# One token tile first through four weight pieces, at two hand-overs of a two-block transformer kernel

## The chip, the cores and the metric

The kernel runs on one core of a Trainium2 chip. The metric is the device time of one execution in microseconds (us). Times of one profiled execution come from the hardware profiler; its engines are PE (TensorE, matrix products and transposes), PEld (its weight loads), DVE (VectorE), ACT (ScalarE), POOL (GpSimd) and SP (SyncE, which issues the transfers).

## The reference

256 tokens of width 1024 go through two blocks. All of it is float32; the kernel splits each operand into a high and a low part and forms three products, so that the result keeps float32 accuracy.

```python
def first_block(...):                        # two layers
    for l in range(DEPTH):
        xn = rms_norm(h, norm_g[l])
        ... = jnp.split(xn @ w_in[l], offsets, axis=-1)
        branches = (dsa_branch(...), mla_branch(...), diff_branch(...), sgu_branch(...), memory_branch(...))
        mixed = sum(sigmoid(merge[:, :, n]) * ((o * silu(gates[:, :, n])) @ w_branch[l, n]) ...)
        h = h + mixed @ w_out[l]
    return rms_norm(h, final_norm_g)

def second_block(x, c, ...):
        ada = c_act @ w_ada[l] + b_ada[l]
        shift_a, scale_a, gate_a, shift_m, scale_m, gate_m = jnp.split(ada, N_ADA, axis=-1)
        h = modulate(rmsnorm(x, g_mix[l]), shift_a, scale_a)
        gq, gk, gv, gr, gg, mq, mk, mv = jnp.split(h @ w_in[l], IN_SPLITS, axis=-1)
        o_gla = ...   # gated linear attention from gq, gk, gv, gr, gg
        o_moba = ...  # block-sparse attention from mq, mk, mv
        x = x + gate_a * (concatenate([o_gla, o_moba], axis=-1) @ w_out[l])
        h = modulate(rmsnorm(x, g_mlp[l]), shift_m, scale_m)
        x = x + gate_m * (square(relu(h @ w_ff1[l])) @ w_ff2[l])
    return rmsnorm(x, g_final)
```

The two places where a new operand needs whole rows of a sum (a norm over 1024 columns) between two weight products are called hand-overs here. Hand-over 1: the product with `w_out` of layer 2, the residual, two norms in a row, and the first product of block 2. Hand-over 2: the product with `w_out_2`, the gated residual, a norm, and the first product with `w_ff1_2`.

## The kernel before

**Pieces.** All weights stream as pieces of 512 rows (4 slices of 128 along K) by up to 512 columns, 1 MB each. SP loads a piece into one of three raw buffers (`load`, L357). `split` (L369 to L389) makes a high part on ACT (L381) and a low part on DVE (L382), each as two half-splits of 128 x 1024; there are four buffers of each kind. `run_stream` splits a piece three pieces ahead of its use and loads it six ahead. With `late` it splits after the piece's matmuls instead of before.

**Units.** The 256 tokens are two token tiles: tile 0 (tokens 0 to 127) and tile 1. `mm_tok` (L427) multiplies one tile with one piece: four products hi x hi (L431) and four with the low part of the weights (L432) in turn, then four with the low part of the tokens (L434), 12 matmuls of 512 columns into one PSUM bank. This is called a unit. A chunk of 512 output columns needs two pieces (K halves) for each of the two tiles, four units.

**The order of units.** An ordinary `chunk` or `chunk_pair` runs both tiles of a piece before the next piece. At the hand-overs the kernel before has two other orders. `chunk_pair(..., by_tile=True)`, for `w_out` of layer 2 (L1224) and `w_out_2` (L1626), runs the first two pieces (first K half, both chunks) in the ordinary order and then the second K half as: chunk 0 tile 0, chunk 1 tile 0, chunk 0 tile 1, chunk 1 tile 1. `chunk_by_tile`, for the first chunk behind each hand-over (gq and gk at L1596, the first 512 columns of `w_ff1_2` at L1708), runs K half 0 tile 0, K half 1 tile 0, then both halves of tile 1. The second 512 columns of `w_ff1_2` are made transposed (`chunk_tr`, L444 to L447, matmuls of 256 columns) and need no transposes; the first are transposed by PE afterwards (L552).

**From rows to operand.** At hand-over 1 a unit's residual is L1183, at hand-over 2 L1608 and L1609; ACT takes the square sum of each half row (`sumsq`, L629); DVE makes the reciprocal root in small steps (L225 to L233) and scales the rows (L1282). `to_operand_mod` (L585) then transposes 8 squares (L552), scales and shifts two of four on ACT (L597) and two on DVE (L595), and splits into high (L598, ACT) and low part (L599, DVE). The gated operand inside `w_out_2` goes through `to_operand` (L566 ACT, L567 DVE).

**What sets the order.** PE, ACT and DVE each run their instructions in the order that the program fixes. That order comes from a scheduler that sees the code's order and priorities (`urgent`, L1287's `SOONER`); `defer(fn, n)` (L311) places work after n more units, and `half` (L315) counts them.

Of the kernel before, what the change touches and what calls it, by code (L numbers as in the profile page):

```python
# [57 lines left out]
def block_kernel(ctx: ExitStack, tc: tile.TileContext, a, out):  # L58
# [414 lines left out]
    def chunk_by_tile(ap, ops, c0, n, evac, pre=None, post=None, mid=None):  # L473

        st = {}

        def f0(hi, lo):
            st["w"] = hi, lo
            st["ps"] = [mbank(), mbank()]
            assert 0 in ops[0]().filled  # L480
            mm_tok(st["ps"][0], ops[0](), 0, hi, lo, 4, n, True, False, 0)
            half(0)

        def f1(hi, lo):
            w = [st["w"], (hi, lo)]
            mm_tok(st["ps"][0], ops[1](), 0, hi, lo, 4, n, False, True, 0)
            evac(0, st["ps"][0][:, :n])
            half(1)
            if mid:
                mid()  # L490
            for j in range(2):
                assert 1 in ops[j]().filled
                mm_tok(st["ps"][1], ops[j](), 0, *w[j], 4, n, j == 0, j == 1, 1)
                if j == 1:
                    evac(1, st["ps"][1][:, :n])
                    if post:
                        post()
                half(j)
# [1276 lines left out]
```

## Time and profile before

| | |
|---|---|
| median of three runs | 1231.11 us (1230.07 to 1232.33) |
| profiled execution | 1232.42 us |
| its span | 1230.5 us |
| PE busy | 1211.6 us, 98% of the span |
| DVE busy | 903.7 us, 73% |
| ACT busy | 664.5 us, 54% |
| mean granted PE clock | 0.99 |
| transfers | 231.30 MB, 188 GB/s on average |

A row of the timeline has a start in us from the start of the span, a duration, the engine, the line, the operation and the names of its output and inputs, and in brackets how long the engine stood idle before and what ended that. Successive matmuls overlap in these rows: the distance between starts, not the duration, is what one costs. "x4" is a run of four. Hand-over 1 lies at about 887 to 917 us, hand-over 2 at about 1020 to 1052 us.

### The profile page before, as it was taken

Reading aid. Unit: us, or ns where it says so; the run is one execution under the profiler, and the core shown is the slowest. Engines: PE = TensorE matmul, PEld = TensorE weight load, DVE = VectorE, ACT = ScalarE, POOL = GpSimd, SP = SyncE. Lnnn points to the kernel's source line nnn. Section 1 sums busy time; section 2 is a strip of 40 time slices with the busy share of each in tenths; the row PEclk is TensorE's granted clock in tenths of the full one; section 3 lists DMA queues with packets and bytes.
Section 4 is the critical chain, followed back from the end, with each engine's and each line's share of the span. In section 5 each row is a group of like instructions: output and inputs, shape, how many; then the busy total and the mean of one; then the engine's idle time right before and its main releaser. Section 6 shows DMA issues by size and latency. Waiting matters only on the chain.

```text
span 1230.5 us, 17201 instructions
## 1 busy us (share of the span) xinstructions
PE 1211.6 (98%) x6497; PEld 1044.2 (85%) x6497; DVE 903.7 (73%) x1887; ACT 664.5 (54%) x1161; POOL 14.8 (1%) x35
## 2 busy tenths in 40 slices
PE   9999999999999999999999999999999999999997
PEld 7799888898888888898888988888878877899995
DVE  6866778768896777776887788876685877757665
ACT  6744645567465455546444756555455655545442
POOL 3000000000000000000000000000000000000000
PEclk9999999999999999999999999999988999999999
DMA  8855465544566465755565535656357724757650
GB/s 303 306 181 199 137 206 189 178 153 156 163 220 205 138 206 186 250 172 171 171 211 192 172 124 189 206 172 218 109 171 265 255 85 163 223 188 243 233 174 35
DMA packets 121284, 231.30 MB, mean 188 GB/s; under 512 B 5421, under 2 KB 17009, under 8 KB 121073
## 3 DMA queue, kind: packets, MB, share of 16 engines
q1 hardware_dynamic: 120880, 230.12, 56.8%
q8 instruction: 51, 0.84, 0.3%
q14 instruction: 33, 0.26, 0.1%
q0 software_dynamic: 320, 0.08, 0.1%
HBM read 229.10 MB, written 2.63 MB: 188 GB/s over the span
## 4 chain that ended last, share of the span: by engine, by line
PE 91%; DVE 4%; ACT 1%; DMA 1%; issue 1%; SPq 0%; ACTq 0%
PE pm L431 22%; PE pm L432 22%; PE pm L434 22%; PE pm L446 3%; PE pm L444 3%; PE pm L447 3%; PE po L703 3%; PE pm L552 3%; DVE wl L382 2%; PE pm L683 2%; DMA wt<-in_w_in_dram 1%; PE pm L1100 1%; PE pm L988 1%; PE pm L851 1%; PE po L434 1%
## 5 line engine op out<-in xcount | busy, mean ns | idle before, releaser
L382 DVE TENSOR_TENSOR wl<-wt,wh 128x1024 fp32r<-128x1024 f32 (+3 forms) x386 | 443.3, 1175 | 174.2 <-ACT wh L381 173.6
L381 ACT ACTIVATE wh<-wt 128x1024 fp32r<-128x1024 f32 (+3 forms) x386 | 379.5, 1019 | 272.1 <-PE pm L434 168.0
L431 PE MATMUL pm<-wh,hi 128*128 128x512 f32 (+4 forms) x1320 | 521.0, 396 | 4.0 <-ACT hi L598 2.6
L432 PE MATMUL pm<-wl,hi 128*128 128x512 f32 (+4 forms) x1320 | 509.5, 387 | 0.0
L434 PE MATMUL pm<-wh,lo 128*128 128x512 f32 (+4 forms) x1320 | 348.0, 384 | 0.0
L431 PEld LDWEIGHTS pm<-wh,hi 128*128 128x128 f32 x1320 | 251.3, 190 | 52.6 <-ACT hi L598 4.7
L432 PEld LDWEIGHTS pm<-wl,hi 128*128 128x128 f32 x1320 | 251.3, 190 | 45.6 <-DVE wl L382 0.6
L434 PEld LDWEIGHTS pm<-wh,lo 128*128 128x128 f32 x1320 | 246.5, 189 | 47.5
L446 PE MATMUL pm<-lo,wh 128*128 128x256 f32 x352 | 99.8, 284 | 2.9 <-DVE lo L580 2.9
L444 PE MATMUL pm<-hi,wh 128*128 128x256 f32 x352 | 100.6, 286 | 0.0
L447 PE MATMUL pm<-hi,wl 128*128 128x256 f32 x352 | 99.6, 284 | 0.0
L656 ACT ACTIVATE w<-w,s 128x256 f32<-128x256 f32 (+1 forms) x112 | 49.9, 446 | 39.0 <-DVE s L653 39.0
L446 PEld LDWEIGHTS pm<-lo,wh 128*128 128x128 f32 x352 | 67.8, 193 | 3.6 <-DVE lo L580 3.1
L444 PEld LDWEIGHTS pm<-hi,wh 128*128 128x128 f32 x352 | 67.9, 193 | 0.3
L447 PEld LDWEIGHTS pm<-hi,wl 128*128 128x128 f32 x352 | 67.7, 192 | 0.1
L1332 DVE SCALAR_TENSOR_TENSOR w<-wt,cact,w 128x512 f32<-128x512 f32 x84 | 62.7, 747 | 1.7 <-DMA wt<-in_w_ada_dram 0.6
L1146 ACT ACTIVATE t<-pm,s 128x512 f32<-128x512 f32 x40 | 27.5, 688 | 43.6 <-PE pm L434 43.6
L703 PEld LDWEIGHTS po<-t,w 128*128 128x128 f32 x352 | 46.0, 191 | 2.9
L552 PE MATMUL pm<-ident,t 128*128 128x128 f32 (+1 forms) x332 | 43.8, 273 | 1.6 <-DVE t L1282 1.6
L703 PE MATMUL po<-t,w 128*128 128x64 f32 (+1 forms) x352 | 44.8, 270 | 0.0
L552 PEld LDWEIGHTS pm<-ident,t 128*128 128x128 f32 (+1 forms) x332 | 38.4, 137 | 7.4 <-issue 2.4
L629 ACT ACTIVATE j<-t 128x512 f32<-128x512 f32 (+3 forms) x60 | 28.8, 479 | 28.1 <-DVE t L1682 14.1
(282 smaller groups left out, 1005.1 us busy)
## 6 DMA issues: line engine op xcount, KB each, us to landing
wt<-in_w_in_dram SPq DMA_DIRECT2D x99, 1024.0 KB, 5.0
wt<-in_w_ff_dram SPq DMA_DIRECT2D x32, 1024.0 KB, 5.4
wt<-in_w_ada_dram SPq DMA_DIRECT2D x24, 1024.0 KB, 5.2
wt<-in_w_branch_dram SPq DMA_DIRECT2D x20, 1024.0 KB, 5.1
wt<-in_w_out_dram SPq DMA_DIRECT2D x12, 1024.0 KB, 5.1
wt<-in_mem_w_kv_dram SPq DMA_DIRECT2D x8, 1024.0 KB, 7.3
wt<-in_w_in_dram SPq DMA_DIRECT2D x4, 904.0 KB, 5.5
wt<-in_w_in_dram SPq DMA_DIRECT2D x4, 768.0 KB, 4.4
```

Source lines behind the costliest of these rows:

```text
L381: pin(A.activation(hv[:, ks], wv[:, ks], AF.Copy), on)
L382: pin(V.tensor_tensor(lv[:, ks], wv[:, ks], hv[:, ks].bitcast(F32), OP.subtract), on)
L431: T.matmul(ps[:, :n], xh, hi[:, i, :n], start=first and i == 0, stop=False)
L432: T.matmul(ps[:, :n], xh, lo[:, i, :n], start=False, stop=False)
L434: T.matmul(ps[:, :n], xo.lo[:, k0 + i, tsl(t)], hi[:, i, :n], start=False, stop=last and i == nk - 1)
L444: T.matmul(ps, wh, xh, start=first and i == 0 and c % 2 == 0, stop=False, skip_group_check=True)
L446: T.matmul(ps, wh, xl, start=False, stop=False, skip_group_check=True)
L447: T.matmul(ps, wl, xh, start=False, stop=last and i == nk - 1, skip_group_check=True)
L552: T.transpose(ps[:, i, :], src[:, i * w:(i + 1) * w], ident)
L656: A.activation(p[:, k, :], p[:, k, :], AF.Exp, bias=mx[:, k:k + 1], scale=-1.0, accum_out=sm[:, k:k + 1])
L703: T.matmul(opsum[t][:, h, :], pt[:, k * nb + b, :], u["v"](h, b), start=b == 0, stop=b == nb - 1)
L1332: V.scalar_tensor_tensor(acc, w[:, i, :], B["c"][:, k:k + 1], acc, op0=OP.mult, op1=OP.add)
```

## The change

Both special orders go. `chunk_pair` gets an `order` of its four pieces; with it, tile 0 goes through all four (both K halves and both chunks), with four units, and the pieces stay in their four split buffers (`keeps`). Then tile 1 goes through the four in the order chunk 0 (both K halves), chunk 1 (both). After each of tile 1's first three units `freed` lets the stream split the next piece. This order is used for `w_out` of layer 2, for gq/gk together with mq in block 2 (so mq moves ahead of the narrow gg), for `w_out_2`, and for the first 1024 columns of `w_ff1_2`; the second 512 of these are now made by tiles and transposed like the first. `modulated` is deferred by five units (it was 3 for tile 0 and 2 for tile 1 at hand-over 1, and 2 at hand-over 2).

```diff
+        at = dict(split=1, load=AHEAD, live=1)
+        def more(i):
+            while at["split"] < min(i + LOOK + 1, N):
+                raw = pieces[at["split"]][5]
+                if not raw and at["live"] > LOOK:
+                    break
+                at["live"] += not raw
+                split(at["split"])
+                at["split"] += 1
+            while at["load"] < min(at["split"] + AHEAD - LOOK, N):
+                load(at["load"])
+                at["load"] += 1
+        def freed():
+            at["live"] -= 1
+            more(at["i"])
+        stream["freed"] = freed
...
-            if i + LOOK < N and not late:
-                split(i + LOOK)
-            if i + AHEAD < N:
-                load(i + AHEAD)
+            _, nk, n, fn, pre, raw, keeps = pieces[i]
+            more(i)
...
-            if i + LOOK < N and late:
-                split(i + LOOK)
+                if not keeps:
+                    at["live"] -= 1
...
+        todo = order or [(j, q) for j in range(2) for q in range(2)]
+        for k, (j, q) in enumerate(todo):
+            def fn(hi, lo, j=j, q=q, k=k):
+                mm(j, q, 0, hi, lo)
+                if not order:
...
+                st["w", j, q] = hi, lo
+                half(k % 2)
+                if k < 3:
+                    return
+                for m, jq in enumerate([(0, 0), (1, 0), (0, 1), (1, 1)]):
+                    mm(*jq, 1, *st["w", *jq])
+                    if m < 3:
+                        stream["freed"]()
+                    elif post:
+                        post()
+                    half(m % 2)
...
-                   pres={(0, 0): lambda: defer(lambda: mixT(1), 1)}, by_tile=l == DEPTH - 1)
+        def second_half():
+            for t in range(2):
+                defer(lambda t=t: mixT(1, (t,)), 1 + t)
+        chunk_pair(a["w_out"][l], mt, [(0, 512), (512, 512)], [eo(0), eo(1)], pres={(0, 0): second_half},
+                   order=[(0, 0), (0, 1), (1, 0), (1, 1)] if l == DEPTH - 1 else None)
...
-            x[t], x[t], rsqrt(m, 1), None, op0=OP.mult)), 3 - t)
+            x[t], x[t], rsqrt(m, 1), None, op0=OP.mult)), 5)
...
-        chunk_by_tile(w2, ops, 0, 512, tok("gqk", 512), pre=block2_begins)
+        chunk_pair(w2, ops, [(0, 512), (1552, 512)], [tok("gqk", 512), tok("mq", 512)], pres={(0, 0): block2_begins},
+                   order=[(0, 0), (0, 1), (1, 0), (1, 1)])
         chunk(w2, ops, 1536, 16, tok("gg", 16), post=lambda: lanes[1].add(gla()))
-        chunk(w2, ops, 1552, 512, tok("mq", 512))
...
-                    defer(modulated(t, r, B["x2"], B["am"], B["bm"]), 2)
+                    defer(modulated(t, r, B["x2"], B["am"], B["bm"]), 5)
...
-                   by_tile=True)
+                   order=[(0, 0), (0, 1), (1, 0), (1, 1)])
...
-        chunk_by_tile(w1, fo, 0, 512, ff1_0)
+        chunk_pair(w1, fo, [(0, 512), (512, 512)], [ff1_by_tile(0), ff1_by_tile(1)],
+                   order=[(0, 0), (0, 1), (1, 0), (1, 1)])
         for f in range(8):
-            if f + 1 < 8:
+            if 0 < f < 7:
                 ff1(f + 1)
             ff2(f)
-            if f == 0:
-                after_norm.update(id(p) for p in pieces[first + 2:first + 4])
```

What the engines' programs look like for it is shown at three places. In these rows a name with a number is one buffer's tile, "[waits ...]" lists the engines or transfer queues that the instruction waits for, and lines of the changed file are two or more higher than before (L383 is L381, L384 is L382, L451 to L454 are L431 to L434, L1707 is L1703; L566, L595 to L599 and L629 keep their numbers).

PE at hand-over 1, before: the last four matmuls of tile 1's last unit (`pm1511`), tile 0's eight transposes, and the first matmul of block 2 (`pm1572`).

```order
L434 MATMUL pm1511_8181<-wh1498_8120,lo1490_8081 128x512 x4
L552 MATMUL pm1559_8360<-ident_81,t1538_8286 128x128 [waits DVE_49,PE_49]
L552 MATMUL pm1559_8360<-ident_81,t1538_8286 128x128
L552 MATMUL pm1560_8365<-ident_81,t1538_8286 128x128 x2
L552 MATMUL pm1562_8373<-ident_81,t1538_8286 128x128 [waits DVE_49]
L552 MATMUL pm1562_8373<-ident_81,t1538_8286 128x128
L552 MATMUL pm1563_8378<-ident_81,t1538_8286 128x128 x2
L431 MATMUL pm1572_8411<-wh1507_8172,hi1515_8227 128x512 [waits Activation_49]
```

PE at the same place now: the third unit of tile 1 ends and the fourth begins (`pm1545`), transposes, the rest of that unit, the first matmul of block 2.

```order
L454 MATMUL pm1545_8304<-wh1481_8052,lo1488_8079 128x512 x4
L451 MATMUL pm1545_8304<-wh1498_8120,hi1489_8080 128x512
L552 MATMUL pm1561_8366<-ident_81,t1529_8242 128x128 [waits DVE_49]
L552 MATMUL pm1561_8366<-ident_81,t1529_8242 128x128
L552 MATMUL pm1562_8371<-ident_81,t1529_8242 128x128 [waits PE_49]
L552 MATMUL pm1562_8371<-ident_81,t1529_8242 128x128
L552 MATMUL pm1564_8379<-ident_81,t1529_8242 128x128 [waits DVE_49]
L552 MATMUL pm1564_8379<-ident_81,t1529_8242 128x128
L552 MATMUL pm1565_8384<-ident_81,t1529_8242 128x128 x2
...
L454 MATMUL pm1545_8304<-wh1498_8120,lo1490_8081 128x512 x4
L451 MATMUL pm1572_8411<-wh1531_8258,hi1507_8185 128x512 [waits Activation_49]
```

The transposes moved from behind tile 1's last unit to one matmul into it, so that eleven matmuls now stand between them and the first matmul that needs ACT's high part.

ACT at hand-over 2, tile 0, before (`hi1798` and `hi1800` are the high halves of the FF operand, `t2` is tile 1's row of the residual, `wh` a weight piece's high part).

```order
L381 ACTIVATE wh1835_9674<-wt1785_9445 128x1024 [waits DMAHW0_49,PE_49]
L381 ACTIVATE wh1835_9674<-wt1785_9445 128x1024
L597 ACTIVATE w1821_9614<-pm1822_9615,adaT_127,s1803_9548 128x128 [waits PE_49]
L597 ACTIVATE w1821_9614<-pm1822_9615,adaT_127,s1803_9548 128x128
L597 ACTIVATE w1824_9627<-pm1825_9628,adaT_127,s1803_9548 128x128 [waits PE_49]
L597 ACTIVATE w1824_9627<-pm1825_9628,adaT_127,s1803_9548 128x128
L629 ACTIVATE j1820_9611,s1818_9609<-t2_88 128x512 [waits DVE_49,Activation_49]
L598 ACTIVATE hi1798_9541<-w1821_9614 128x4x128 [waits DVE_49,Activation_49]
L381 ACTIVATE wh1837_9680<-wt1792_9493 128x1024 [waits DMAHW1_49,PE_49]
L629 ACTIVATE j1830_9657,s1828_9655<-t2_88 128x512 [waits DVE_49,Activation_49]
L381 ACTIVATE wh1837_9680<-wt1792_9493 128x1024
L598 ACTIVATE hi1800_9543<-w1824_9627 128x4x128 [waits DVE_49]
```

ACT at the same place now (`hi1790` and `hi1792` are the high halves).

```order
L383 ACTIVATE wh1820_9612<-wt1785_9445 128x1024 [waits DMAHW0_49,PE_49]
L383 ACTIVATE wh1820_9612<-wt1785_9445 128x1024
L383 ACTIVATE wh1837_9680<-wt1811_9569 128x1024 [waits DMAHW1_49,PE_49]
L597 ACTIVATE w1831_9654<-pm1832_9655,adaT_127,s1795_9506 128x128 x2
L597 ACTIVATE w1834_9667<-pm1835_9668,adaT_127,s1795_9506 128x128
L629 ACTIVATE j1826_9637,s1824_9635<-t2_88 128x512 [waits DVE_49,Activation_49]
L598 ACTIVATE hi1790_9499<-w1831_9654 128x4x128 [waits DVE_49,Activation_49]
L597 ACTIVATE w1834_9667<-pm1835_9668,adaT_127,s1795_9506 128x128
L383 ACTIVATE wh1837_9680<-wt1811_9569 128x1024
L598 ACTIVATE hi1792_9501<-w1834_9667 128x4x128 [waits DVE_49,Activation_49]
```

The first half-split of `wh1837`, which stood behind the first high half, now stands ahead of the L597, and the L629 ahead of the first L598 is the one of the second half row (`j1826`), where it was the first half row's (`j1820`).

ACT right behind that, for tile 1, before.

```order
L597 ACTIVATE w1842_9702<-pm1843_9703,adaT_127,s1803_9548 128x128 [waits PE_49]
L597 ACTIVATE w1842_9702<-pm1843_9703,adaT_127,s1803_9548 128x128
L597 ACTIVATE w1845_9715<-pm1846_9716,adaT_127,s1803_9548 128x128 [waits PE_49]
L597 ACTIVATE w1845_9715<-pm1846_9716,adaT_127,s1803_9548 128x128
L598 ACTIVATE hi1798_9541<-w1842_9702 128x4x128 [waits DVE_49,Activation_49]
L1703 ACTIVATE w1851_9744<-pm1840_9688 128x512 [waits PE_49]
L598 ACTIVATE hi1800_9543<-w1845_9715 128x4x128 [waits DVE_49,Activation_49]
```

ACT for tile 1 now.

```order
L1707 ACTIVATE w1844_9728<-pm1840_9688 128x512 [waits PE_49]
L1707 ACTIVATE w1848_9746<-pm1841_9701 128x512 [waits PE_49]
L566 ACTIVATE hi1842_9726<-pm1856_9776 128x4x128 [waits PE_49]
L597 ACTIVATE w1850_9750<-pm1851_9751,adaT_127,s1795_9506 128x128 x2
L597 ACTIVATE w1853_9763<-pm1854_9764,adaT_127,s1795_9506 128x128 [waits DVE_49]
L597 ACTIVATE w1853_9763<-pm1854_9764,adaT_127,s1795_9506 128x128
L598 ACTIVATE hi1790_9499<-w1850_9750 128x4x128 [waits DVE_49,Activation_49]
L598 ACTIVATE hi1792_9501<-w1853_9763 128x4x128 [waits DVE_49,Activation_49]
```

Two evacuations of tile 0's FF units and the high part of their transposes now stand ahead of tile 1's high halves.

## Rows read from the trace of the kernel before

**Rows 1.** The page: busy time, share of the span, instructions of each engine.

```profile
PE 1211.6 (98%) x6497; PEld 1044.2 (85%) x6497; DVE 903.7 (73%) x1887; ACT 664.5 (54%) x1161; POOL 14.8 (1%) x35
```

**Rows 2.** The page: the chain that ended last, share of the span.

```profile
PE 91%; DVE 4%; ACT 1%; DMA 1%; issue 1%; SPq 0%; ACTq 0%
```

**Rows 3.** PE's waits, 880 to 1064 us: total us, times, longest.

```profile
PE pm L431 <- ACT hi L598: 2.6, 3, 1.2
PE pm L552 <- DVE t L1282: 1.6, 2, 1.4
```

**Rows 4.** Timeline of PE at hand-over 1.

```profile
889.90 0.39 PE L431 MATMUL pm<-wh,hi 128*128 128x512 f32 x1
...
892.62 0.39 PE L431 MATMUL pm<-wh,hi 128*128 128x512 f32 x1
...
897.66 1.07 PE L434 MATMUL pm<-wh,lo 128*128 128x512 f32 x4
900.12 1.06 PE L552 MATMUL pm<-ident,t 128*128 128x128 f32 x8 [1.40 <-DVE t L1282]
902.30 0.79 PE L431 MATMUL pm<-wh,hi 128*128 128x512 f32 x1 [1.11 <-ACT hi L598]
...
905.78 1.08 PE L434 MATMUL pm<-wh,lo 128*128 128x512 f32 x4
```

**Rows 5.** Windows: length; busy PE, PEld, DVE, ACT, POOL; granted clock; DMA.

```profile
901.00:904.00 3.00, 1.89 (x6) 1.41 (x5) 2.93 (x13) 2.92 (x8) 0.00 (x0) 0.70 1.04 365
...
1037.00:1039.00 2.00, 0.83 (x5) 0.36 (x3) 2.00 (x6) 2.00 (x7) 0.00 (x0) 1.00 0.00 0
...
919.00:922.00 3.00, 3.00 (x18) 3.00 (x17) 2.33 (x3) 0.89 (x2) 0.00 (x0) 0.55 0.93 169
```

**Rows 6.** Timeline of PE at hand-over 2.

```profile
1035.82 1.06 PE L552 MATMUL pm<-ident,t 128*128 128x128 f32 x8 [0.20 <-DVE t L1282]
...
1038.97 0.50 PE L431 MATMUL pm<-wh,hi 128*128 128x512 f32 x1 [1.17 <-ACT hi L598]
...
1046.22 0.50 PE L431 MATMUL pm<-wh,hi 128*128 128x512 f32 x1 [0.28 <-ACT hi L598]
...
1052.35 0.28 PE L446 MATMUL pm<-lo,wh 128*128 128x256 f32 x1
1052.47 0.28 PE L447 MATMUL pm<-hi,wl 128*128 128x256 f32 x1
```

**Rows 7.** Groups by line and form, 860 to 1064 us: busy, mean ns, idle before.

```profile
L382 DVE TENSOR_TENSOR wl<-wt,wh 128x1024 fp32r<-128x1024 f32 x53 | 63.2, 1219 | 21.0 <-ACT wh L381 20.9
...
L566 ACT ACTIVATE hi<-pm 128x512 fp32r<-128x512 f32 x10 | 5.5, 594 | 3.4 <-PE pm L552 3.4
```

**Rows 8.** Timeline of DVE at hand-over 2.

```profile
1026.78 2.36 DVE L382 TENSOR_TENSOR wl<-wt,wh 128x1024 fp32r<-128x1024 f32 x2 [3.22 <-ACT wh L381]
...
1031.12 0.69 DVE L1608 TENSOR_TENSOR w<-pm,t 128x512 f32<-128x512 f32 x1 [0.66 <-PE pm L434]
...
1035.18 0.88 DVE L1282 TENSOR_SCALAR t<-t,s 128x512 f32<-128x512 f32 x2
...
1036.59 0.40 DVE L595 TENSOR_SCALAR w<-pm,s,adaT 128x128 f32<-128x128 f32 x1
```

**Rows 9.** Timeline of ACT at hand-over 2.

```profile
1032.64 0.63 ACT L629 ACTIVATE j<-t 128x512 f32<-128x512 f32 x1 [1.35 <-DVE t L1609]
...
1033.84 2.01 ACT L381 ACTIVATE wh<-wt 128x1024 fp32r<-128x1024 f32 x2 [0.48 <-PE pm L434]
1036.27 1.50 ACT L597 ACTIVATE w<-pm,adaT,s 128x128 f32<-128x128 f32 x4 [0.41 <-PE pm L552]
1037.68 0.63 ACT L629 ACTIVATE j<-t 128x512 f32<-128x512 f32 x1
...
1038.31 0.61 ACT L598 ACTIVATE hi<-w 128x512 fp32r<-128x512 f32 x1
```

**Rows 10.** The page: issues of transfers, KB each, us to landing.

```profile
wt<-in_w_ff_dram SPq DMA_DIRECT2D x32, 1024.0 KB, 5.4
```

More of the change, by code (lines that the diff above doesn't have):

```diff
@@ L327, in half, with piece @@
             lanes[2].step()
-    pieces, pinned, after_norm = [], [], set()
-    def piece(src, nk, n, fn, pre=None, raw=False, late=False):
-        pieces.append([src, nk, n, fn, pre, raw, late])
+    pieces, pinned = [], []
+    stream = {}
+    def piece(src, nk, n, fn, pre=None, raw=False, keeps=False):
+        pieces.append([src, nk, n, fn, pre, raw, keeps])
     def spread(first, fns):
@@ L386, in split @@
                 return part
-            with behind(("xn", 1), id(pieces[i]) in after_norm):
-                for k in range(0, nk, 2):
-                    part(k, 2, pieces[i] in pinned)
+            for k in range(0, nk, 2):
+                part(k, 2, pieces[i] in pinned)
         load(0)
@@ L406, in run_stream @@
         pinned.extend(pieces[1:LOOK])
-        for i in range(1, LOOK):
-            split(i)
+        at = dict(split=1, load=AHEAD, live=1)
[14 more added lines that the diff above has]
+        stream["freed"] = freed
+        more(-1)
         for i in range(N):
+            at["i"] = i
             if i == 1:
@@ L414, in run_stream @@
                 silu_c()
-            _, nk, n, fn, pre, raw, late = pieces[i]
-            if i + LOOK < N and not late:
-                split(i + LOOK)
-            if i + AHEAD < N:
-                load(i + AHEAD)
+            _, nk, n, fn, pre, raw, keeps = pieces[i]
+            more(i)
             if pre:
@@ L471, in chunk, with chunk_pair @@
             piece(wsrc(ap, r0 + j * 512, 4, c0, n), 4, n, fn, pre if j == 0 else None)
[L473 to L498, printed above, removed]
-        piece(wsrc(ap, 0, 4, c0, n), 4, n, f0, pre)
-        piece(wsrc(ap, 512, 4, c0, n), 4, n, f1, late=True)
-    def chunk_pair(ap, ops, cols, evacs, pres=None, post=None, rows=(0, 512), by_tile=False):
+    def chunk_pair(ap, ops, cols, evacs, pres=None, post=None, rows=(0, 512), order=None):
         st = {}
@@ L1173, in mixT @@
                 L["mT"] = [Operand(), Operand()]
-            for t in range(2):
+            for t in ts:
                 to_operand(mixed[t][:, j * 512:(j + 1) * 512], t, L["mT"][j], scale=0.25)
@@ L1673, in fn @@
                         half(k % 2)
-                piece(wsrc(wf, f * 512, 4, c * 512, 512), 4, 512, fn, late=f == 7 and c == 1)
+                piece(wsrc(wf, f * 512, 4, c * 512, 512), 4, 512, fn, keeps=f == 7 and c == 0)
         @urgent
```

53 lines of the change are left out of this document (22 added, 31 removed).

## The prediction

> **What bounds the kernel now.** I read the shares by engine first, then the chain that ended last, then the waits of the matmul engine (PE) between 880 and 1064 us, and only then the timelines of the two hand-overs, because the change touches nothing else. The first two show a kernel that is PE from end to end: PE is busy for 1211.6 of 1230.5 us [rows 1] and has 91% of the chain [rows 2]. So a change can only win where PE stands still or runs slowly, and it loses wherever it makes PE wait. The waits give the size of the prize: in the stretch that holds both hand-overs PE waits 2.6 us for high halves of the next operand (L598) and 1.6 us for normalized rows (L1282) [rows 3], 4.2 us together.
>
> One unit is 12 matmuls of 512 columns for one token tile and one weight piece. It takes 892.62 - 889.90 = 2.72 us, 0.227 us a matmul [rows 4].
>
> Hand-over 1 before: after the last unit of tile 0 and two units of tile 1 PE waits 1.40 us for L1282, makes eight transposes, and waits 1.11 us for L598 [rows 4]. Behind that its granted clock is 0.70 of full in a stretch of 3 us [rows 5], a mix of the two levels (2.4 and 1.2 GHz): the eight matmuls from 902.30 to 905.78 take 3.48 us where 8 x 0.227 = 1.82 would do, 1.66 us lost [rows 4]. Sum of what can be won there: 1.40 + 1.11 + 1.66 = 4.2 us.
>
> Hand-over 2 before: waits of 0.20, 1.17 and 0.28 us, 1.65 together [rows 6], and the clock stays at 1.00 [rows 5].
>
> **The change part by part.** Now tile 0 goes through four pieces, then tile 1 through the same four. Behind tile 0's last unit stand four units of tile 1, 4 x 2.72 = 10.9 us of PE work in which tile 0's next operand can be made; before, two stood there. No piece, transfer or product is added. That is the good half. The other half: four pieces held until tile 1 has used them leave no buffer for the next four, so their splits, and the transfers behind these, come in a burst in those same 10.9 us, on the two engines that also make the operand. I count T from the end of tile 0's last unit; at hand-over 2 tile 1's units end at 2.7, 5.4, 9.0 (eight transposes, 0.8 us, stand inside the third) and 11.7; at hand-over 1 two ada rows of 0.46 us make that 2.7, 5.4, 8.6 and 12.2, with the transposes inside the fourth.
>
> *Hand-over 1.* Three half-splits (L382) now stand inside VectorE's chain to L1282. The first can run when tile 1's first unit has given up its buffer and ScalarE has made its half: 2.7 + 1.0 = 3.7 (two take 2.01 [rows 9]). Then 3 x 1.22 [rows 7], a residual 0.69 [rows 8], three small steps of 0.2 and half of L1282's 0.88 [rows 8]: 9.1. PE comes to the transposes at 8.6 + 0.23 = 8.8. Wait 0.3, and 0.1 more at their second half: 0.4 (0 to 1.4). The high half follows on ScalarE behind a split that needs the third unit's buffer, a square sum and four L597: 8.6 + 2.01 + 0.63 + 1.50 + 0.66 = 13.4 [rows 6, 9]; PE is there at 12.5: 0.9 (0 to 1.7). Tile 1's transposes find VectorE late by the four splits: about 0.6, my estimate. Sum 1.9 us against 4.2 with the slow matmuls: **-2.3 us**, bounds -4.2 (no wait left) and 0.
>
> *Hand-over 2, first unit of the next pair.* Here ScalarE's own order decides. Before the first high half (L598) of tile 0 now stand, in this order, the split of the third next piece, one half of the split of the fourth, three L597, and a square sum (L629) of tile 1. This square sum needs the residual of tile 1's last unit, so nothing of the 10.9 us covers it. Two bounds from rows:
> - Floor. From the end of tile 1's last unit: L1608 to the start of L629 takes 1032.64 - 1031.12 = 1.52 us [rows 8, 9], one L595 between them 0.40 [rows 8], L629 with its read-out 0.63 (1037.68 to 1038.31), L598 to the matmul 0.66 (1038.31 to 1038.97) [rows 6, 9]. Sum 3.2 us. Before, a square sum of tile 1 also stood ahead of L598 [rows 9], but that of its first half row, from a unit that had ended earlier.
> - With the queues. The fourth piece's transfer can start only when VectorE has split the first piece. L1282 ends 1035.18 + 0.88 - 1031.12 = 4.9 after the residual starts [rows 8]; two half-splits of 1.22 with a residual's 0.6 between them end at 8.0. The transfer takes 5.4 us [rows 10], to 13.4. Then half a split on ScalarE, 1.0, three L597 at 0.37 (1.50 for four), L629 0.63 and L598 0.66 [rows 9]: 16.8 against 11.7.
>
> The wait is 3.2 to 5.1 us, or 6 if the transfer takes longer; I take 5.1, since each term of the longer chain has a row.
>
> *Tile 1's transposes* come after that unit and two matmuls, 3.2 us after it starts. Their L1282 waits for the square sum, one half-split, the low half (L599), another half-split, the next low half and four small steps. With L598's end at 0: ScalarE makes one L597, the second half-split and the next L598 by 1.9, and VectorE's remainder of about 3 us ends at about 5. Wait 1.8 (0.7 to 2.0).
>
> *Second tile of the pair.* Its L598 now stands on ScalarE behind two L1703, the second of which waits for the end of tile 0's last FF unit, behind L566, which waits for four transposes after that, and behind four L597. From that unit's end: 0.5 + 0.5 + 1.5 + 0.66, less the four transposes (0.35) in which PE works, is 2.8; with start-up 2.9 (2.6 to 3.2). Before, no evacuation of a later unit stood ahead of this L598, and it cost 0.28 [rows 6].
>
> *Inside w_out_2* the transposes of the gated operand now stand right before the unit that reads them, with nothing in between but ScalarE's L566, 0.59 [rows 7]: 0.65 (0.2 to 0.7).
>
> Sum 5.1 + 1.8 + 2.9 + 0.65 = 10.45, less the 1.65 of before: **+8.8 us**, bounds 3.2 + 0.7 + 2.6 + 0.2 - 1.65 = +5.0 and 6 + 2.0 + 3.2 + 0.7 - 1.65 = +10.3.
>
> *FF columns 512 to 1023* change from matmuls of 256 columns (96, 0.12 us apart: 1052.47 - 1052.35 [rows 6]) to 48 of 512 at 0.227 and eight transposes: 11.5 against 10.9 + 0.8. I take 0 (-0.5 to +0.5).
>
> *Clock.* At hand-over 1, 902.30 - 898.73 = 3.57 us without a matmul of 512 columns preceded the half clock [rows 4]; at hand-over 2 the wait of 1.17 did not lower it [rows 5, 6]. The wait of 5.1 us should, at the 1.66 us that this cost before, but that falls in the unit after which PE waits 1.8 anyway: 0. The wait of 2.9 is with the transposes about 3.3 us long, close to the known case: half a chance of 1.66, **+0.8**, bounds 0 and 3.3.
> The Trainium skill, "TensorE: Matmul & The Clock Gate", section "Why this matters for your kernels", speaks against the change here: it asks that there be no long gaps between bursts of matmuls, or the engine returns to its lower clock. By that rule both waits would cost, and the sum would be 1.7 to 2.5 us higher; the trace agrees for the longer gap of hand-over 1 and shows no fall behind the shorter one of hand-over 2.
>
> The narrow piece (gg, 16 columns) has the half clock before (0.55 [rows 5]) and moves behind mq unchanged: 0.
>
> **Sum:** -2.3 + 8.8 + 0 + 0.8 = +7.3 on the profiled execution's 1232.42, 1239.7. That execution is 1.3 above the median of the runs, 1231.11, so I forecast 1238.4. Bounds: -4.2 + 5.0 - 0.5 + 0 = +0.3 and 0 + 10.3 + 0.5 + 3.3 = +14.1; not all ends come together, so 1233 to 1244.5 for this case.
>
> **Rivals.**
> 1. *The four units hide it all.* If the operand of tile 0 is made within the 10.9 us, every wait of both hand-overs and the slow matmuls go: -(4.2 + 1.65) = -5.8, 1225.3. It decides whether L598 waits behind the last residual's square sum. For it: at hand-over 2 the normalized rows are there 4.9 us after the unit that they need, and PE asks for them at 5.7. Against: the order of ScalarE at hand-over 2, where the square sum stands first, and a half-split ahead of it that waits for a transfer.
> The Trainium skill, same page, section "HAM oscillation — how this bites in real kernels", recommends this very order, all K tiles for one tile of rows before a wait for transfers, to keep the clock up. By it the 1.66 us come back and this rival is the right one. No row shows PE waiting for a transfer at a hand-over: it waits for ScalarE and VectorE [rows 3], of which the rule does not speak.
> 2. *Only the floor is paid.* The fourth piece lands early and VectorE keeps up: +5.0 at hand-over 2, -4.2 at hand-over 1, clock 0: +0.8, 1231.9, no change that can be told. For it: VectorE is idle 3.22 us before 1026.78 [rows 8] and may be ahead. Against: the transfer can't start before the first piece is split.
> 3. *The clock falls in each gap.* Both long waits lower it, 1.66 us each, and the waits come out at their upper ends with nothing won at hand-over 1: +14.1, less some cover, about +12: 1243 to 1245. For it: hand-over 1 before. Against: the waits themselves hide part of it.
>
> **How the numbers follow.** A measurement of this kernel tells 0.2%, 2.5 us, from no change. Forecast (1233 to 1244.5) 0.68; rival 1 0.10; rival 2 0.10, of which 0.02 comes out slower; rival 3 0.12. Faster 0.10, same 0.08, slower 0.68 + 0.02 + 0.12 = 0.82. The range of 8 in 10 leaves out rival 1 and the end of rival 3: 1230 to 1245.
>
> **What would show it.** In the profile after, PE's waits should list L598 with two waits near 5 and 3 us around the first FF pieces, and L1282 with one near 2; ScalarE should show a half-split (L383 there) idle for a transfer just ahead of three L597. At hand-over 1 the waits of 1.40 and 1.11 should be down to 0.4 and 0.9 with the clock at 1.00. I am wrong if the first FF unit starts within 3 us of the last unit of w_out_2, or if hand-over 1 still shows the half clock.

## The result and the profile after

After: 1246.63 us median of four runs (1244.27 to 1248.06), against 1231.67 of four runs before. The ratio is 1.0121 (95% interval 1.0106 to 1.0136): 15 us slower, outside the predicted range of 1230 to 1245. The profiled execution took 1246.59 us, 14.2 above the one before; its span is 1244.5, 14.0 above.

In the page after, the rows that answer to [rows 1] and [rows 2] show PE busy 4.4 us longer with no product added, so it ran slower somewhere, and it stands idle for 28.5 us instead of 18.9 (span less busy time). Of the chain, PE has 2 points less.

```profile
PE 1216.0 (98%) x6457; PEld 1045.3 (84%) x6457; DVE 903.6 (73%) x1887; ACT 664.0 (53%) x1161; POOL 14.9 (1%) x35
...
PE 89%; DVE 5%; DMA 2%; ACT 2%; issue 1%; SPq 0%; ACTq 0%; DVEq 0%
```

PE's waits after, 860 to 1100 us (total us, times, longest), against [rows 3]:

```profile
PE pm L451 <- ACT hi L598: 8.3, 3, 5.0
PE pm L683 <- ACT w L656: 2.4, 2, 2.0
PE pm L1454 <- DVE w L1450: 2.0, 1, 2.0
PE pm L451 <- ACT hi L566: 0.7, 1, 0.7
PE po L703 <- DVE w L687: 0.4, 1, 0.4
PE pm L552 <- DVE t L1562: 0.4, 1, 0.4
```

The first row holds both hand-overs. L1282's waits are gone. The next rows are new, and three of them lie in neither hand-over: L683 transposes the probabilities of o_moba (MoBA here, fed by the exponentials of L656), L703 multiplies by them, and L1454 reads the gate of o_gla (GLA here, copied by L1450). The rows of L566 and L1562 stand inside w_out_2: L1562 is the last step of GLA's result, and L566 makes the high part of the operand from it.

**Hand-over 1**, PE's timeline after, against [rows 4]:

```profile
896.18 1.09 PE L552 MATMUL pm<-ident,t 128*128 128x128 f32 x8
...
900.44 0.50 PE L451 MATMUL pm<-wh,hi 128*128 128x512 f32 x1 [0.65 <-ACT hi L598]
```

The transposes no longer wait (1.40 before), the first unit waits 0.65 (1.11 before).

**Hand-over 2**, PE's timeline after, against [rows 6]:

```profile
1040.39 1.07 PE L454 MATMUL pm<-wh,lo 128*128 128x512 f32 x4
1046.41 0.80 PE L451 MATMUL pm<-wh,hi 128*128 128x512 f32 x1 [4.95 <-ACT hi L598]
...
1049.99 1.91 PE L454 MATMUL pm<-wh,lo 128*128 128x512 f32 x4
...
1052.32 1.03 PE L552 MATMUL pm<-ident,t 128*128 128x128 f32 x8
...
1064.19 0.50 PE L451 MATMUL pm<-wh,hi 128*128 128x512 f32 x1 [2.65 <-ACT hi L598]
```

And ACT's, against [rows 9]:

```profile
1038.87 1.99 ACT L383 ACTIVATE wh<-wt 128x1024 fp32r<-128x1024 f32 x2
1043.13 1.06 ACT L383 ACTIVATE wh<-wt 128x1024 fp32r<-128x1024 f32 x1 [2.27 <-DMA wt<-in_w_ff_dram]
1044.09 1.14 ACT L597 ACTIVATE w<-pm,adaT,s 128x128 f32<-128x128 f32 x3
1045.12 0.63 ACT L629 ACTIVATE j<-t 128x512 f32<-128x512 f32 x1
1045.73 0.63 ACT L598 ACTIVATE hi<-w 128x512 fp32r<-128x512 f32 x1
```

Read ACT's rows downwards: two half-splits, 2.27 us idle for a transfer, the half-split that waited for it, three L597, the square sum, and only then the high half that PE waits for.

**Between them**, PE's timeline after in the attention stage. None of these waits stood there before. The first row, L1448, makes the gate's transposes, which the copy L1450 reads:

```profile
930.39 0.63 PE L1448 MATMUL pm<-ident,t 128*16 128x128 f32 x2
...
946.06 1.97 PE L1454 MATMUL pm<-w,w 16*128 16x256 f32 x4 [1.97 <-DVE w L1450]
947.96 1.97 PE L552 MATMUL pm<-ident,t 128*128 128x128 f32 x8
...
968.29 0.44 PE L683 MATMUL pm<-ident,w 128*128 128x128 f32 x2 [2.01 <-ACT w L656]
```

What PE waits for stands on DVE. DVE after, in the same stretch:

```profile
942.99 2.36 DVE L384 TENSOR_TENSOR wl<-wt,wh 128x1024 fp32r<-128x1024 f32 x2 [5.43 <-ACT wh L383]
...
945.60 0.41 DVE L1450 COPY w<-pm 16x256 f32<-16x256 f32 x1
...
960.51 1.22 DVE L384 TENSOR_TENSOR wl<-wt,wh 128x1024 fp32r<-128x1024 f32 x1
...
967.11 0.42 DVE L653 CUSTOM_DVE_ANT_0 w<-pm,t 128x256 f32<-128x256 f32 x1
```

The gate copy L1450 stands behind two half-splits before which DVE was idle for 5.43 us. Its input was made 15 us earlier, at 930.39: here DVE's order makes the copy late. L653, the row maximum ahead of MoBA's exponentials, stands behind three half-splits and steps of an ada row. In DVE's timeline before, the copy (then L1447) went ahead of the half-split:

```profile
932.80 0.41 DVE L1447 COPY w<-pm 16x256 f32<-16x256 f32 x1 [11.48 <-PE pm L1445]
933.14 1.20 DVE L382 TENSOR_TENSOR wl<-wt,wh 128x1024 fp32r<-128x1024 f32 x1
```

**The clock**, windows after (columns as in [rows 5]; the granted clock stands behind POOL's figure):

```profile
900.00:905.00 5.00, 4.56 (x18) 3.01 (x19) 5.00 (x7) 3.46 (x6) 0.00 (x0) 1.00 0.11 17
...
945.00:950.00 5.00, 3.94 (x13) 3.11 (x14) 4.55 (x11) 2.49 (x4) 0.00 (x0) 0.62 0.66 211
950.00:955.00 5.00, 5.00 (x21) 4.04 (x21) 3.81 (x5) 4.92 (x7) 0.00 (x0) 0.70 0.66 210
1045.00:1050.00 5.00, 3.59 (x9) 2.82 (x10) 4.31 (x12) 3.17 (x7) 0.00 (x0) 0.52 0.60 210
...
1065.00:1070.00 5.00, 5.00 (x18) 4.03 (x17) 0.95 (x2) 1.51 (x2) 0.00 (x0) 0.66 0.00 0
```

Hand-over 1 now has the full clock. Half clock (1.2 GHz) stands behind the gate's wait and behind both waits of hand-over 2. It also stands behind the narrow piece gg, for a shorter stretch than before.

**Where the 14.2 us went.** PE's waits, and the time lost to half clock by the distance between starts of its matmuls against 0.227 us, place by place, after less before:

| place | waits | half clock | sum | forecast |
|---|---|---|---|---|
| hand-over 1 | -1.9 | -1.7 | -3.5 | -2.3 |
| narrow piece gg | 0 | -1.7 | -1.7 | 0 |
| attention stage and the operand in w_out_2 | +5.7 | +3.5 | +9.2 | +0.65 |
| hand-over 2 | +5.95 | +4.2 | +10.2 | +8.15 and 0.8 for the clock |

### The profile page after: what moved, and what is told of

It reads as the page before. It is cut to its first block, busy times and chain, and to the rows that moved or that the text cites. A ratio compares the mean times of both kernels' runs of the same rounds, so it can differ in the third digit from the quotient of the medians.

```text
span 1244.5 us, 17131 instructions
## 1 busy us (share of the span) xinstructions
PE 1216.0 (98%) x6457; PEld 1045.3 (84%) x6457; DVE 903.6 (73%) x1887; ACT 664.0 (53%) x1161; POOL 14.9 (1%) x35
## 4 chain that ended last, share of the span: by engine, by line
PE 89%; DVE 5%; DMA 2%; ACT 2%; issue 1%; SPq 0%; ACTq 0%; DVEq 0%
PE pm L451 22%; PE pm L452 22%; PE pm L454 22%; PE pm L466 3%; PE pm L467 3%; PE pm L464 3%; PE po L703 3%; PE pm L552 3%; DVE wl L384 2%; PE pm L683 2%; DMA wt<-in_w_in_dram 1%; PE pm L1100 1%; PE pm L988 1%; PE pm L851 1%; PE po L454 1%
## 5 line engine op out<-in xcount | busy, mean ns | idle before, releaser
L384 DVE TENSOR_TENSOR wl<-wt,wh 128x1024 fp32r<-128x1024 f32 (+4 forms) x386 | 444.1, 1176 | 181.7 <-ACT wh L383 180.9
L451 PE MATMUL pm<-wh,hi 128*128 128x512 f32 (+3 forms) x1336 | 527.9, 397 | 10.4 <-ACT hi L598 8.3
L383 ACT ACTIVATE wh<-wt 128x1024 fp32r<-128x1024 f32 (+4 forms) x386 | 379.3, 1018 | 260.5 <-PE pm L454 149.8
L452 PE MATMUL pm<-wl,hi 128*128 128x512 f32 (+3 forms) x1336 | 516.0, 387 | 0.0
L454 PE MATMUL pm<-wh,lo 128*128 128x512 f32 (+3 forms) x1336 | 353.1, 385 | 0.0
L451 PEld LDWEIGHTS pm<-wh,hi 128*128 128x128 f32 x1336 | 254.0, 190 | 59.2 <-ACT hi L598 9.3
L454 PEld LDWEIGHTS pm<-wh,lo 128*128 128x128 f32 x1336 | 250.2, 189 | 48.8
L466 PE MATMUL pm<-lo,wh 128*128 128x256 f32 x320 | 90.7, 284 | 2.8 <-DVE lo L580 2.8
L464 PE MATMUL pm<-hi,wh 128*128 128x256 f32 x320 | 91.3, 286 | 0.0
L467 PE MATMUL pm<-hi,wl 128*128 128x256 f32 x320 | 90.7, 284 | 0.0
L656 ACT ACTIVATE w<-w,s 128x256 f32<-128x256 f32 (+1 forms) x112 | 49.8, 446 | 35.6 <-DVE s L653 35.6
L466 PEld LDWEIGHTS pm<-lo,wh 128*128 128x128 f32 x320 | 61.6, 193 | 3.4 <-DVE lo L580 3.0
L464 PEld LDWEIGHTS pm<-hi,wh 128*128 128x128 f32 x320 | 61.8, 193 | 0.3
L703 PEld LDWEIGHTS po<-t,w 128*128 128x128 f32 x352 | 45.8, 191 | 3.4 <-DVE w L687 0.6
L629 ACT ACTIVATE j<-t 128x512 f32<-128x512 f32 (+3 forms) x60 | 28.8, 479 | 34.9 <-DVE t L1685 14.1
L703 PE MATMUL po<-t,w 128*128 128x64 f32 (+1 forms) x352 | 44.9, 270 | 0.4 <-DVE w L687 0.4
```

Source lines behind the costliest of these rows:

```text
L383: pin(A.activation(hv[:, ks], wv[:, ks], AF.Copy), on)
L384: pin(V.tensor_tensor(lv[:, ks], wv[:, ks], hv[:, ks].bitcast(F32), OP.subtract), on)
L451: T.matmul(ps[:, :n], xh, hi[:, i, :n], start=first and i == 0, stop=False)
L452: T.matmul(ps[:, :n], xh, lo[:, i, :n], start=False, stop=False)
L454: T.matmul(ps[:, :n], xo.lo[:, k0 + i, tsl(t)], hi[:, i, :n], start=False, stop=last and i == nk - 1)
L464: T.matmul(ps, wh, xh, start=first and i == 0 and c % 2 == 0, stop=False, skip_group_check=True)
```

## The experiments

Theory A: the row that the forecast lacks comes from hand-over 1's part, which puts mq ahead of gg, so that GLA starts a chunk (four units, 10.9 us) later; hand-over 2 costs what ACT's order there says. Theory B: hand-over 1's part only wins, and all else belongs to hand-over 2's part. Line numbers shift by some 30 between these kernels; the names tell which instruction it is. The ratios can differ by some 0.1% from those of the medians beside them.

### Each hand-over alone

Hand-over 1 alone (hand-over 2 in the order before):

```diff
-                   order=[(0, 0), (0, 1), (1, 0), (1, 1)])
+                   by_tile=True)                      # w_out_2, with the deferral of 2
...
-        chunk_pair(w1, fo, [(0, 512), (512, 512)], ...)
+        chunk_by_tile(w1, fo, 0, 512, ff1_by_tile(0))
```

> The change at hand-over 1 alone: w_out of layer 2 in the four-piece order and gq/gk paired with mq, hand-over 2 as in the kernel before. Theory A, from the two traces: hand-over 1 itself wins 3.5 us, the narrow piece 1.6 us, but mq ahead of gg costs 8.0 us in the attention stage behind it (a wait of 2.0 us for the gate copy, 3.4 us of half clock behind that, 2.8 us of waits in MoBA's softmax), so +2.9 us, about 1234.6. Rival B, the loss in the attention stage has nothing to do with hand-over 1 (it comes with the four-piece order of w_out_2 behind it, or differs from run to run): -5.1 us, about 1226.6.

1238.03 us against 1231.44, ratio 1.0053 (1.0038 to 1.0068). PE waits 3.6 us for MoBA's exponentials, 2.0 for the gate and 0.7 + 0.4 inside w_out_2; hand-over 1 itself 0.64. Hand-over 2 got worse too, though it has its old order here: 0.40 and 2.54 us instead of 1.65 in all, with half clock behind the longer wait, some 2.8 us together:

```profile
1044.12 0.50 PE L452 MATMUL pm<-wh,hi 128*128 128x512 f32 x1 [2.54 <-ACT hi L630]
```

Hand-over 2 alone (w_out and gq/gk in the order before, `defer(modulated(...), 3 - t)` there):

> The change at hand-over 2 alone: w_out_2 and the first 1024 columns of w_ff1_2 in the four-piece order, hand-over 1 as before. Theory A: waits of 5.0, 2.7, 0.7 and 0.4 us in place of 1.65, and 4.5 us of half clock behind the two long ones: +11.5 us, about 1243.2. The prediction's own terms would give +9.6, about 1241.3. Rival B (the attention stage's 8 us belong to this part): +19.5 us, about 1251.

1239.84 us, ratio 1.0066 (1.0051 to 1.0081). The waits at hand-over 2 are 4.97 and 2.65; in the attention stage there is one of 0.2, as before, and inside w_out_2 none. The two differences, 6.6 and 8.4, add up to the 15.0 of the whole change. B falls. A had the first 3.4 too low and the second 3.4 too high. The waits inside w_out_2, for which the prediction had a cause at hand-over 2, belong to hand-over 1's part: GLA ends late. The 2.8 at hand-over 2's old order stand in the first difference as well, though the whole change hasn't that order; that the two add up so well is in part luck.

### Hand-over 2: ACT's order

```diff
-                    defer(modulated(t, r, B["x2"], B["am"], B["bm"]), 5)
+                    defer(modulated(t, r, B["x2"], B["am"], B["bm"]), 3)
```

> As e2, with the operand of the FF product deferred by three units in place of five, which puts both tiles' high halves on ScalarE ahead of the last square sum and of all FF evacuations. Theory A (ScalarE's order makes the waits, not the amount of work in the burst of splits): the wait of 5.0 us falls to 1 or less, that of 2.7 to about 0.5, and the clock stays up: about +1 us against the kernel before, 1232.5. Rival (the burst of four splits and the fourth piece's transfer hold ScalarE up whatever the order): waits of at least 3 and 2 us with half clock stay, about 1239 to 1243.

Hand-over 2 alone with this one number: 1231.08 us, ratio 0.9999 (0.9989 to 1.0008), 8.8 below the kernel that defers by 5. ACT's timeline there (L628 is the shift and scale, L660 the square sum, L629 the high half):

```profile
1033.29 1.06 ACT L383 ACTIVATE wh<-wt 128x1024 fp32r<-128x1024 f32 x1 [1.96 <-PE pm L454]
1034.26 1.49 ACT L628 ACTIVATE w<-pm,adaT,s 128x128 f32<-128x128 f32 x4
1035.62 0.64 ACT L660 ACTIVATE j<-t 128x512 f32<-128x512 f32 x1
...
1036.23 0.64 ACT L629 ACTIVATE hi<-w 128x512 fp32r<-128x512 f32 x1
```

The half-split ahead of L628 now waits for a split buffer (PE's L454), no longer for a transfer, and the high half is written at 1036.23 instead of 1040.82 in the kernel that defers by 5. At this hand-over the wait of 4.97 goes, the half clock goes, and of the 2.65 a wait of 1.53 is left, now for DVE. Nothing else was changed, so the place at which the operand's steps stand, not the order of the units, cost this hand-over its 8 us. (The number also moves PE's transposes and DVE's norm; that ACT's order is what counts is read from the rows, not tried alone.) The order of units alone wins nothing there.

### Hand-over 1: where the lost lead is paid

Two kernels try to take away the waits of hand-over 1 alone where they stand. The first puts mv ahead of mk, so that MoBA starts later. The second starts the gate's step a turn later and spreads two ada rows from four pieces further on.

```diff
-        chunk(w2, ops, 2064, 512, tok("mk", 512), post=after_mk)
         chunk(w2, ops, 2576, 512, tok("mv", 512))
+        chunk(w2, ops, 2064, 512, tok("mk", 512), post=after_mk)
...
+        yield                                # the other kernel: behind the gate copy
-        spread(first + 5, [lambda: ada(4, ("ga", 0)), lambda: ada(5, ("ga", 1))])
+        spread(first + 9, [lambda: ada(4, ("ga", 0)), lambda: ada(5, ("ga", 1))])
```

> As e1, with the chunk mv ahead of the chunk mk, so that MoBA, which starts behind mk, again starts two chunks behind gg, as before the change. Theory A1 (MoBA started too early beside GLA): the 2.8 us of waits in MoBA's softmax go, the wait for the gate copy and the half clock behind it (5.4 us) stay: +0.3 us against the kernel before, about 1232. Theory A2 (all of the attention stage's loss is the lost lead): -5.1 us, about 1226.6. Rival (the order of these chunks doesn't matter): as e1.

1240.91 us, ratio 1.0087 (1.0067 to 1.0106), above every number expected. MoBA's 3.6 fall to 0.7 and hand-over 2 is as before the change, but PE waits 1.2 for ScalarE's copy of a product and pays at w_out_2 for MoBA's end, with half clock (eight transposes in 1.97 us):

```profile
1016.76 1.97 PE L584 MATMUL pm<-ident,t 128*128 128x128 f32 x8 [3.05 <-DVE t L755]
```

> As e1, with two things taken off VectorE's queue where PE waited: the gate product L1454 comes one unit later behind its copy, and the two ada pieces (L1335) come four pieces later. Theory A1 (VectorE's fixed queue makes the waits): the wait of 2.0 us goes, that of 3.1 falls to 1.5 or less: 1233 to 1235. Rival A2 (GLA's lost lead makes them: what is bought here is paid later in the stage): about as e1, 1237 to 1239.

1236.96 us, ratio 1.0041 (1.0026 to 1.0057). The gate's wait is gone (the copy runs at 934.93, right behind its transposes) and MoBA's is 1.2, but now GLA's end is late at w_out_2, and hand-over 2 waits 0.3 and 2.55 again:

```profile
1019.01 1.05 PE L584 MATMUL pm<-ident,t 128*128 128x128 f32 x4 [2.97 <-DVE t L1595]
```

Both moved the wait and won nothing that can be told from the first kernel. A better slot in DVE's order takes the gate's wait away, but the time is lost again where GLA or MoBA must be done. That speaks for a lost lead of GLA and MoBA over PE.

### Hand-over 1: w_out's order and the pair apart

The order of w_out alone, with gq/gk, gg and mq as before:

> Only w_out of layer 2 in the four-piece order; the products behind it as before the change: gq/gk by tiles, then gg, then mq (tile 1's operand deferred by three units, since it is needed two units earlier than in the pair). Theory A (mq ahead of gg makes the loss behind hand-over 1): the attention stage stays as before; hand-over 1 wins its 3.5 us but pays a wait of about 3 us for tile 1's rows, which now have only two units of cover: about 1231, 1229 to 1232. Rival (the four-piece order of w_out delays the attention stage by itself): 1236 or more.

1236.02 us, ratio 1.004 (1.0027 to 1.0054); a miss. It is the rival's number without the rival's cause: the attention stage has no wait but the 0.2 of before. PE waits for the transfer of the relative bias, which SP issues at 904.04 us, behind pieces that now go out together (901.67 before), and which PE asks for at 906.5 (910.4 before). Half clock stands from 908.9 to 919.1 us, and from 925.9 to 932.8 at gg, there shorter than before (919.3 to 929.5):

```profile
910.05 1.43 PE L1404 MATMUL pm<-w,w 32*8 32x384 f32 x2 [3.54 <-DMA w<-in_rel_bias_dram]
```

The pair of gq/gk and mq alone, with w_out in the order before:

> Only the pair of gq/gk with mq (mq ahead of gg); w_out of layer 2 and hand-over 2 as before the change. Theory A: the loss behind hand-over 1 comes whole, without the gain of w_out's order: e1's 6.6 + 3.5 = +10 us, 1239 to 1241, with the wait for the gate copy (2.0) and for MoBA's softmax (about 3) in the trace. Rival: no such waits, 1231 to 1233.

1243.07 us, ratio 1.0087 (1.007 to 1.0103). Its size is some 3 above what was expected, but its place is another. By waits and half clock some 7 us of it lie at hand-over 1, 3 at hand-over 2 (waits of 0.40 and 2.54, half clock from 1050.9) and 2 between them. At hand-over 1 PE waits 6.20 us for L1315, and DVE's timeline shows why:

```profile
902.10 1.22 DVE L384 TENSOR_TENSOR wl<-wt,wh 128x1024 fp32r<-128x1024 f32 x1
...
903.43 1.21 DVE L384 TENSOR_TENSOR wl<-wt,wh 128x1024 fp32r<-128x1024 f32 x1
...
905.30 0.88 DVE L1315 TENSOR_SCALAR t<-t,s 128x512 f32<-128x512 f32 x2
```

With w_out as before only two units of tile 1 cover this work, and four half-splits stand in it. The gate had no wait here and MoBA 0.2, against A, though PE was also slow behind gg (half clock from 938.2 to 948.5), which left GLA more time. So the two halves of hand-over 1's change do not add up (5.1 + 12.2 against 6.6 together), and neither alone tests A. The next run does.

### Only gg's place

Hand-over 1 alone, with gg as gq/gk's partner and mq behind, as before:

```diff
-        chunk_pair(w2, ops, [(0, 512), (1552, 512)], [tok("gqk", 512), tok("mq", 512)], ...)
-        chunk(w2, ops, 1536, 16, tok("gg", 16), post=lambda: lanes[1].add(gla()))
+        chunk_pair(w2, ops, [(0, 512), (1536, 16)], [tok("gqk", 512), tok("gg", 16)], ...,
+                   post=lambda: lanes[1].add(gla()), order=[(0, 0), (0, 1), (1, 0), (1, 1)])
+        chunk(w2, ops, 1552, 512, tok("mq", 512))
```

> As e1, but gq/gk is paired with the narrow gg in place of mq, and mq follows: GLA again starts four units earlier and MoBA two chunks behind it. Theory A: the waits for the gate copy and MoBA's softmax go, hand-over 1 keeps its gain of 3.5 us (tile 1's rows have about 8 us of cover, and two narrow pieces in the burst of splits): about 1228. Rival (the loss belongs to the four-piece order itself): 1236 or more.

1225.68 us against 1230.88, ratio 0.9946 (0.9928 to 0.9964): 11.8 us better than with mq as partner, when each is held against the runs of the kernel before beside it. PE's waits, 860 to 1100 us:

```profile
PE pm L452 <- ACT hi L630: 2.9, 3, 1.5
PE pm L584 <- DVE t L1318: 0.2, 1, 0.2
PE pm L1580 <- DVE w L1563: 0.2, 1, 0.2
```

Gate, MoBA and w_out_2's operand no longer wait. By place, against hand-over 1 alone, some 8 us are won in the attention stage and w_out_2, 3.4 at the narrow piece, which has the full clock here, and 2.8 at hand-over 2; 0.8 are lost to a longer wait for tile 1's high half at hand-over 1.

So the loss comes with mq as partner, as A has it. But two things change with the partner: GLA starts four units earlier, and the burst of splits is shorter, since two of the four pieces are now narrow (the two half-splits of such a piece take DVE 0.32 us, those of a wide one 2.36).

No run parts the two, but the traces speak for the start of GLA. In the kernel after, DVE had worked the burst off before gg was done; it stood idle ahead of its next wide half-split, and the gate's transposes come at 930.39:

```profile
925.99 2.79 DVE L384 TENSOR_TENSOR wl<-wt,wh 128x1024 fp32r<-128x1024 f32 x2 [6.44 <-ACT wh L383]
```

And in each of the six kernels with mq ahead of gg, PE waits inside w_out_2 for the end of GLA or MoBA (0.7 to 3.1 us at the longest), in none of the eight with gg first.

The whole change with that swap alone, with the deferral of 3 alone, and with both:

> The change with only the partner of gq/gk swapped (gg in place of mq, mq behind). Additive: e7's 1225.7 + e2's 8.4 = 1234.1, that is 12.5 us below the change. Rival (half of e1's loss is bound to the order of the units, not to the partner): above 1238.

> The change with only the FF operand's deferral at three units. Additive: 1246.6 - 8.8 = 1237.8, the same as e1. Rival (with the late end of GLA the high halves wait anyway): above 1241.

> The change with both mends: gq/gk paired with gg in place of mq (e7), and the FF operand deferred by three units in place of five (e4). If the two hand-overs' shares add up: e7's 1225.7 and e4's 0, about 1225.5 (1223 to 1228). Rival (the four-piece order at hand-over 2 costs something that e4 could hide only because GLA and MoBA ended earlier there): 1229 or more.

| | deferral 5 | deferral 3 |
|---|---|---|
| partner mq | 1246.63 (1.0121) | 1233.53 (1.0017; 1.0004 to 1.0029) |
| partner gg | 1235.01 (1.0034; 1.0021 to 1.0046) | 1225.25 (0.9959; 0.9944 to 0.9973) |

The last one beats the kernel before by 0.4%; it has 1.5 + 1.5 + 0.2 us of waits left between 860 and 1100 us. Hand-over 1 alone with gg as partner was as fast (0.9946), so the new order at hand-over 2 adds nothing even when mended. The deferral alone came 4 us lower than the sum of its parts, with the waits for the gate (2.0) and MoBA (2.4) still there. In its trace 3.4 us of that are clock: the half clock behind gg (930.6 to 934.1 us) and behind the gate's wait (947.7 to 951.1) is half as long as in the kernel after (929.1 to 936.0 and 946.2 to 953.0). Nothing that the deferral moves stands there, so it is not shown to be its doing.

### The kernel before with gg's pieces between mq's

The kernel with gg as partner had the full clock at gg. Theory C: narrow pieces that alternate with wide ones keep the clock, whatever else is done.

```diff
-        chunk(w2, ops, 1536, 16, tok("gg", 16), post=lambda: lanes[1].add(gla()))
-        chunk(w2, ops, 1552, 512, tok("mq", 512))
+        chunk_pair(w2, ops, [(1536, 16), (1552, 512)], [gg_then_gla, tok("mq", 512)])
```

> The kernel before the change with one edit: the narrow pieces gg alternate with the wide pieces of mq (first K half of gg, of mq, second half of gg, of mq) in place of all of gg ahead of mq. Theory C (48 narrow matmuls in a row let the clock fall, and e7's gain is in large part that it breaks this row up): the half clock around the narrow piece goes, 4.9 us, and GLA starts one unit pair later: 1226 to 1228. Rival (e7's gain is the new order at hand-over 1): 1230.5 to 1232.

1232.48 us, ratio 1.0008 (0.9997 to 1.0018): no change. Each of the two narrow pieces (24 matmuls of 16 columns in a row) is followed by half clock, at 921 and 931 us, for shorter stretches than before, and the waits for high halves come to 3.9 us instead of 2.6. C falls: alternating alone does not keep the clock here, and the gain of gg as partner needs more of hand-over 1's order than that.

## Why the prediction was wrong

The direction was right, at 0.82, and the size was half of what came.

1. *Hand-over 1, -2.3: right, a little low.* Waits 0 and 0.65 against 0.4 and 0.9, full clock as said: -3.5.
2. *Hand-over 2's first unit, 5.1: right.* 4.95, by the chain that was worked out: transfer, half-split, three L597, square sum, high half. The deferral of 3 takes that chain apart and wins the 8 us back.
3. *Second tile of the pair, 2.9: right.* 2.65.
4. *Tile 1's transposes, 1.8: wrong.* They did not wait, because the unit before them ran at half clock: 14 matmuls, 1046.41 to 1052.32, took 5.9 us where 14 x 0.227 = 3.2 would do. At full clock PE would have asked at 1049.6, and DVE began the norm's scaling for them at 1050.64, so a wait near the forecast was there to be had. The 2.7 lost stand in the clock's account instead, and the sign "L1282 with one near 2" did not come.
5. *Clock, +0.8: too small.* The prediction let the fall behind the long wait cost nothing and gave the 2.65 half a chance of 1.66. Both fell, 2.7 and 1.5 us. The Trainium skill, "TensorE: Matmul & The Clock Gate", section "Why this matters for your kernels", asks for no long gaps between bursts of matmuls; the trace after agrees at 4.95 us. At 2.65 us the traces go both ways: half clock here, full clock behind the same wait in the whole change with gg as partner (last section). So half a chance was a fair guess for that wait.
6. *"The narrow piece (gg, 16 columns) ... moves behind mq unchanged: 0": this step failed, and it is the largest.* The piece itself took 1.7 us less. But GLA is started by gg's last unit, and behind mq that is a chunk later. GLA and MoBA then came nearer to each other and to PE: gate, softmax and w_out_2's operand made PE wait 5.9 us, and 3.5 more went to half clock. Swapping the partner alone brings back 11 to 12 us (1238.03 to 1225.68, and 1246.63 to 1235.01); that is more than 9.2 because it also wins at other places, above all clock. I had counted the matmuls of the moved piece and not what is started behind it. That the late start does it, and not the longer burst of splits that comes with mq as partner, is read from the traces and was not tried alone.
7. *Inside w_out_2, 0.65: right in size, wrong in cause.* The wait of 0.69 is there, but with hand-over 2's part alone it is not, and with hand-over 1's alone it is: GLA's end, point 6. That the size fits is luck.

Rival 1 (the four units hide all) came true for the transposes of hand-over 1 alone. Rival 2 (only the floor is paid) fell: ACT's half-split stood idle 2.27 us for the fourth piece. Rival 3, the clock falling in each gap, was right for hand-over 2 and not for hand-over 1. Its 1243 to 1245 came nearest, but by luck: it wins nothing at hand-over 1, where 3.5 us were won, and it lacks the 9.2 of the attention stage, as every rival does.

What stays open: why the two halves of hand-over 1's change cost 5.1 and 12.2 alone and 6.6 together (each has a wait of its own, for the bias and for L1315, which the other's presence takes away, but that was not tried one by one); why hand-over 2 in its old order waits longer in three kernels with mq as partner; and why the clock came back sooner in the kernel with the deferral of 3 beside mq.

## What to carry to other kernels

Where a change moves a piece, list what its last instruction starts, and follow that work to the place where the main engine needs its result: the moved matmuls here cost nothing, and in the stage behind them 9 us were lost. An engine that runs in fixed order makes the one that waits for it pay for whatever stands ahead of the awaited instruction; look there first, since a single number of deferral was worth 8.8 us. When a wait is taken away where it shows and the time stays, look for it at the next place where the same chain is awaited.

## What the runs showed of the hardware

The same narrow matmuls can be followed by either clock. In the kernel with gg as partner and in the one with both mends, PE does the same from 914 us on: wide matmuls, 24 narrow ones without a gap, wide ones. The first goes on at full clock, the second at half:

```profile
918.08 0.59 PE L455 MATMUL pm<-wh,lo 128*128 128x16 f32 x4
918.53 0.49 PE L452 MATMUL pm<-wh,hi 128*128 128x512 f32 x1
918.85 0.40 PE L453 MATMUL pm<-wl,hi 128*128 128x512 f32 x1
```

and in the other:

```profile
917.79 0.59 PE L454 MATMUL pm<-wh,lo 128*128 128x16 f32 x4
918.23 0.67 PE L451 MATMUL pm<-wh,hi 128*128 128x512 f32 x1
918.70 0.63 PE L452 MATMUL pm<-wl,hi 128*128 128x512 f32 x1
```

A wait of 1.97 us for the gate was followed by half clock in the kernel after (four matmuls of L1454 in 1.97 us) and by the full clock in hand-over 1 alone, where the same four took 1.13 us. The wait of 2.65 us at hand-over 2 was followed by half clock in the kernel after and by the full clock in the whole change with gg as partner, where the next matmuls start 0.23 us apart:

```profile
1053.98 0.50 PE L451 MATMUL pm<-wh,hi 128*128 128x512 f32 x1 [2.65 <-ACT hi L598]
1054.32 0.40 PE L452 MATMUL pm<-wl,hi 128*128 128x512 f32 x1
1054.55 0.40 PE L451 MATMUL pm<-wh,hi 128*128 128x512 f32 x1
```

So a stretch of this kind costs nothing or, at the places above, 1.5 to 3.5 us, and the trace of one kernel doesn't tell which it will be in the next. Executions of one kernel differ in it too: the four of hand-over 1 alone with gg as partner took 1223.8, 1224.5, 1226.9 and 1227.1 us at mean granted clocks of 0.998, 0.997, 0.994 and 0.995. The us of half clock by place are therefore those of the profiled executions.
